# A load-and-store-bound SiLU-gate kernel: loads moved to the ACT ring, stores to the SP ring, with program order kept in every queue

## The chip, the cores and the metric

One core of one Trainium2 chip. The metric is the device time of one execution in microseconds (us), as the median of several runs. The profile's own span is about 1.8 us shorter than the time of the same run (470.1 against 471.92 us), so spans are compared with spans and times with times.

Words used below: SP, ACT and DVE are three engines of the core; in this kernel ACT computes the SiLU, DVE multiplies, and SP only issues transfers. A *ring* (or queue) is the list of transfers that one issuing engine feeds; here there are two, one fed by SP and one by ACT. A *piece* is one of the four 1 MB stores into which the last tile's output is cut. *Landing* is the moment when a transfer's completion is seen. Tiles are numbered 0 to 15, pieces 0 to 3.

## The reference

```python
batch, seq, dim = (32, 512, 2048)                 # x: float32, 134.2 MB
x1, x2 = x[..., :1024], x[..., 1024:]
out = (x1 * (1 / (1 + np.exp(-x1))) * x2)         # float32, 67.1 MB
```

There is nothing to reuse: 134.22 MB must be read and 67.11 MB written.

## The kernel before

The rows are cut into 16 tiles of 1024 rows (128 partitions with 8 rows each). Two input buffers and two output buffers rotate. SP issues the loads and ACT the stores. ACT computes SiLU of the left half, DVE multiplies by the right half, in four chunks per tile. The last tile's store is cut into four pieces so that it can start before the whole tile is done.

```python
    K = 8
    KC = 2
    # [cut: shapes, pools with bufs=2 for xt and for ot, views xv and ov]
    def load(i):
        xt = in_pool.tile([P, K, in_cols], dt, name="xt")
        nc.sync.dma_start(out=xt, in_=xv[i])
        loaded[i] = xt

    load(0)
    load(1)
    for i in range(n_tiles):
        xt = loaded.pop(i)
        last = i == n_tiles - 1
        ot = out_pool.tile([P, K, half], dt, name="ot")
        for c in range(0, K, KC):
            ce = c + KC
            nc.scalar.activation(                      # L56
                out=ot[:, c:ce, :],
                in_=xt[:, c:ce, :half],
                func=mybir.ActivationFunctionType.Silu,
            )
            nc.vector.tensor_mul(                      # L61
                out=ot[:, c:ce, :],
                in0=ot[:, c:ce, :],
                in1=xt[:, c:ce, half:],
            )
            if last:
                nc.scalar.dma_start(out=ov[i][:, c:ce, :], in_=ot[:, c:ce, :])   # L67
        if not last:
            nc.scalar.dma_start(out=ov[i], in_=ot)     # L69
        if i + 2 < n_tiles:
            load(i + 2)                                # L45
```

This order in the source is not the order on the engines: a scheduler places the instructions. In the built program the last tile stands on ACT as three activations, three store pieces, the fourth activation, the fourth piece.

## Time and profile before

| | before |
|---|---|
| time, median of 3 runs | 472.03 us (471.82 to 472.82) |
| span of the profiled run | 470.1 us |
| DVE busy, ACT busy | 30%, 25% of the span |
| period of one tile in the middle | 29.0 us |
| DMA rate in the middle | 434 GB/s |

From the page of the kernel before: busy time by engine, the DMA row of the timeline (tenths of 16 engines in 40 slices), the queues (packets, MB, share of the time of 16 engines), and the chain that ended last.

```profile
DVE 142.4 (30%) x64; ACT 118.3 (25%) x65; POOL 0.2 (0%) x4
...
DMA  8999999999999999999999999999999999999998
...
q1 hardware_dynamic: 2304, 134.22, 66.2%
q10 hardware_dynamic: 2736, 67.11, 33.1%
q14 instruction: 2, 0.02, 0.0%
...
DMA 80%; DVE 15%; ACT 4%; issue 0%; ACTq 0%; SPq 0%
```

Two queues with 66.2% and 33.1% add up to 99.3%: the 16 DMA engines have work for all but about 3 us of the span. q1 carries the loads (134.22 MB) and belongs to SP, q10 the stores and belongs to ACT.

The view by stretches of the kernel before (columns: stretch, its length, busy time of DVE, ACT and POOL with counts, clock, DMA share, GB/s):

```profile
58.00:116.00 58.00, 17.80 (x8) 14.62 (x8) 0.00 (x0) 1.00 1.00 434
...
290.00:348.00 58.00, 17.80 (x8) 14.62 (x8) 0.00 (x0) 1.00 1.00 434
...
452.00:470.10 18.10, 8.99 (x4) 7.42 (x4) 0.00 (x0) 1.00 0.84 357
```

In the middle the DMA engines move 434 GB/s with share 1.00. The Trainium skill, "DMA: Bandwidth & Descriptors", section "Where 436 GB/s comes from", states a fabric ceiling of 435 GB/s; the 434 GB/s measured here lie just under it. After the first 58 us (414 to 419 GB/s) there is slack only once the last load has landed (452 us).

The timeline of that tail, kernel before (start us, length, engine, line, operation; in brackets the idle time before it and what ended it):

```profile
452.05 5.51 ACT L56 ACTIVATE ot<-xt 128x2048 f32<-128x2048 f32 x3 [21.65 <-DMA xt<-in_x_dram]
453.99 6.70 DVE L61 TENSOR_TENSOR ot<-ot,xt 128x2048 f32<-128x2048 f32 x3 [20.06 <-ACT ot L56]
456.32 4.74 ACTq L67 DMA_DIRECT2D out_dram<-ot  x3
461.11 1.91 ACT L56 ACTIVATE ot<-xt 128x2048 f32<-128x2048 f32 x1 [3.54 <-DVE ot L61]
463.05 2.29 DVE L61 TENSOR_TENSOR ot<-ot,xt 128x2048 f32<-128x2048 f32 x1 [2.36 <-ACT ot L56]
465.37 0.34 ACTq L67 DMA_DIRECT2D out_dram<-ot  x1
```

The fourth activation stands behind the third store piece, and that piece waits for the third multiply. So ACT idles 3.54 us and DVE 2.36 us in the last tile.

The same view by quarter microseconds around the end of piece 2 (kernel before):

```profile
464.75:465.00 0.25, 0.25 (x1) 0.00 (x0) 0.00 (x0) 1.00 1.08 459
465.00:465.25 0.25, 0.25 (x1) 0.00 (x0) 0.00 (x0) 1.00 0.48 197
465.25:465.50 0.25, 0.09 (x1) 0.00 (x0) 0.00 (x0) 1.00 0.23 98
465.50:465.75 0.25, 0.00 (x0) 0.00 (x0) 0.00 (x0) 1.00 0.16 66
465.75:466.00 0.25, 0.00 (x0) 0.00 (x0) 0.00 (x0) 1.00 0.08 33
466.00:466.25 0.25, 0.00 (x0) 0.00 (x0) 0.00 (x0) 1.00 0.55 229
```

There is a hole from 465.1 to 466.2 us, before the data of piece 3 start. In the packet records the first of the 16 engines is done with piece 2 at 465.00 us and the last at 466.14, and they all start piece 3 between 466.21 and 466.36. So the first engine idles for 1.2 to 1.4 us, the last for 0.1 to 0.2.

### The profile page before, as it was taken

The page shows a single profiled execution, that of the slowest core. Times are in us where ns is not written, and L with a number is a line of the kernel's source. Part 1 is how long each engine was busy: PE and PEld are TensorE (multiplying, and loading weights), DVE is VectorE, ACT ScalarE, POOL GpSimd, SP SyncE. Part 2 cuts the span into 40 slices and gives each one's busy share as a digit, 9 for nine tenths or more (in the row PEclk, how much of TensorE's full clock was granted, in tenths as well). Part 3 has the DMA queues.
Part 4 walks back from the last instruction along what each step waited for, and adds up shares of the span by engine and source line. Part 5 has one row for each costly group of instructions (what it writes and reads, how often), then busy time and mean ns, then how long its engine had stood idle before and what let it go on. Part 6 is the DMA issues. An engine that isn't in the chain of part 4 may idle for free.

```text
span 470.1 us, 267 instructions
## 1 busy us (share of the span) xinstructions
DVE 142.4 (30%) x64; ACT 118.3 (25%) x65; POOL 0.2 (0%) x4
## 2 busy tenths in 40 slices
DVE  0070704207052070511606115070250702407033
ACT  1050506014060240602306032060320604106041
POOL 0000000000000000000000000000000000000000
DMA  8999999999999999999999999999999999999998
GB/s 357 446 446 401 401 485 435 418 401 443 449 446 401 441 457 396 446 474 390 468 404 438 457 441 407 427 420 449 446 410 432 480 401 418 440 474 424 399 424 337
DMA packets 5042, 201.35 MB, mean 428 GB/s; under 512 B 560, under 2 KB 560, under 8 KB 560
## 3 DMA queue, kind: packets, MB, share of 16 engines
q1 hardware_dynamic: 2304, 134.22, 66.2%
q10 hardware_dynamic: 2736, 67.11, 33.1%
q14 instruction: 2, 0.02, 0.0%
HBM read 134.22 MB, written 67.11 MB: 428 GB/s over the span
## 4 chain that ended last, share of the span: by engine, by line
DMA 80%; DVE 15%; ACT 4%; issue 0%; ACTq 0%; SPq 0%
DMA xt<-in_x_dram 80%; DVE ot L61 15%; ACT ot L56 4%; SPq L45 0%; ACTq L67 0%; ACTq L56 0%
## 5 line engine op out<-in xcount | busy, mean ns | idle before, releaser
L61 DVE TENSOR_TENSOR ot<-ot,xt 128x2048 f32<-128x2048 f32 x64 | 142.4, 2286 | 322.9 <-ACT ot L56 322.9
L56 ACT ACTIVATE ot<-xt 128x2048 f32<-128x2048 f32 x64 | 117.1, 1898 | 344.0 <-DMA xt<-in_x_dram 340.4
L56 ACT ACT_TABLE_LOAD x1 | 1.3, 1283 | 0.7 <-PEq L86 0.7
L86 POOL MEMSET const-bfloat16-1.0<- 128x1 bf16 x1 | 0.1, 101 | 0.0
L86 POOL MEMSET const-uint8-127<- 128x1 uint8 x1 | 0.1, 101 | 0.0
L86 POOL MEMSET const-float32-0.0<- 128x1 f32 x1 | 0.1, 98 | 0.2 <-issue 0.2
L86 POOL MEMSET const-float32-1.0<- 128x1 f32 x1 | 0.1, 98 | 0.0
## 6 DMA issues: line engine op xcount, KB each, us to landing
out_dram<-ot ACTq DMA_DIRECT2D x15, 4096.0 KB, 39.7
out_dram<-ot ACTq DMA_DIRECT2D x4, 1024.0 KB, 5.4
xt<-in_x_dram SPq DMA_DIRECT2D x16, 47.1
```

What stands on the lines that cost most here:

```text
L56: nc.scalar.activation(out=ot[:, c:ce, :], in_=xt[:, c:ce, :half], func=mybir.ActivationFunctionType.Silu,)
L61: nc.vector.tensor_mul(out=ot[:, c:ce, :], in0=ot[:, c:ce, :], in1=xt[:, c:ce, half:],)
L86: nc = _bacc.Bacc("TRN2", target_bir_lowering=False, num_devices=1)
```

## The change: its intent and the diff

Intent: ACT, which would otherwise be held by the last tile's stores, issues the loads instead (all issued by then), and SP issues the stores. The scheduler is switched off (`manual_schedule`), so each queue keeps program order, and the last tile's pieces follow on the store ring without holding ACT. The `PLAN` code is a general form of the same tiling; with this plan every tile still has 8 rows per partition.

```diff
-    n_tiles = num_rows // (P * K)
+    PLAN = [K] * (num_rows // (P * K))
 [cut: plan and view() compute the same row ranges from PLAN]
+    ctx.enter_context(tc.manual_schedule())
     def load(i):
         xt = in_pool.tile([P, K, in_cols], dt, name="xt")
-        nc.sync.dma_start(out=xt, in_=xv[i])
+        nc.scalar.dma_start(out=xt[:, :plan[i][1], :], in_=view(x_flat, i))
 [cut: unchanged compute]
             if last:
-                nc.scalar.dma_start(out=ov[i][:, c:ce, :], in_=ot[:, c:ce, :])
+                nc.sync.dma_start(out=ov[:, c:ce, :], in_=ot[:, c:ce, :])
         if not last:
-            nc.scalar.dma_start(out=ov[i], in_=ot)
+            nc.sync.dma_start(out=ov, in_=ot[:, :k, :])
```

More of the change, by code (lines that the diff above doesn't have):

```diff
@@ L31, with view @@
     KC = 2
-    n_tiles = num_rows // (P * K)
-    assert n_tiles * P * K == num_rows
+    PLAN = [K] * (num_rows // (P * K))
     in_pool = ctx.enter_context(tc.tile_pool(name="in_pool", bufs=2))
     out_pool = ctx.enter_context(tc.tile_pool(name="out_pool", bufs=2))
-    xv = x_flat.rearrange("(n p k) d -> n p k d", p=P, k=K)
-    ov = out_flat.rearrange("(n p k) d -> n p k d", p=P, k=K)
+    plan = []
+    row = 0
+    for k in PLAN:
+        plan.append((row, k))
+        row += P * k
+    assert row == num_rows
+    n_tiles = len(plan)
+    def view(flat, i):
+        row0, k = plan[i]
+        return flat[row0:row0 + P * k].rearrange("(p k) d -> p k d", k=k)
+    ctx.enter_context(tc.manual_schedule())
     loaded = {}
@@ L50 @@
     for i in range(n_tiles):
+        k = plan[i][1]
         xt = loaded.pop(i)
         last = i == n_tiles - 1
+        ov = view(out_flat, i)
         ot = out_pool.tile([P, K, half], dt, name="ot")
-        for c in range(0, K, KC):
-            ce = c + KC
+        for c in range(0, k, KC):
+            ce = min(c + KC, k)
             nc.scalar.activation(
```

## The prediction

> **What bounds the kernel now.** The 16 DMA engines. The view by stretches gives a DMA share of 1.00 and 434 GB/s in every 58 us pair of tiles from 58 to 406 us. DVE is busy 30%, ACT 25% (the page, part 1); the chain of waits is 80% load transfers. The Trainium skill, "DMA: Bandwidth & Descriptors", section "Where 436 GB/s comes from", gives a fabric ceiling of 435 GB/s; this trace sits on it. So only time in which the DMA engines have nothing to move can be won: about 1 us at the start, and something after the last load lands (452.0 us); from there to 470.1 the mean is 357 GB/s.
>
> **What the change moves.** The order of instructions on each engine shows loads going from SP to ACT and stores from ACT to SP, each still released by the fourth multiply of a tile (in the trace, load and store are issued at 405.10 and 405.11 us). No new wait is real: each store waits for its completion slot of four tiles earlier, long landed. An issue costs 0.33 us on SP, 0.36 us on ACT; ACT then idles about 21 us per tile for its load, so this is hidden. The same page, section "Issuing engines are not separate DMA queues", says that DMAs of either engine run on the same 16 engines; the steady state should keep 29.0 us per tile, loads landing in 47.1 us and stores in 39.6 us, the two queues' bytes exchanged.
>
> **Where it changes something: the last tile.** Before, ACT runs three activations, holds in the three store issues (456.32 to 461.06 us; the third waits for DVE) and starts its fourth activation at 461.11. So the last multiply ends only at 465.34. After, ACT runs four activations straight and SP issues the pieces: DVE multiplies back to back (8.91 us, as for other tiles) and ends at about 462.9, 2.4 us earlier. Not all of that counts: after the last load the store queue still holds the rest of tile 14's store, and the view by quarter microseconds shows the DMA engines full from 458 to 465.1 with that and the first three pieces. Only the hole from 465.2 to about 466.05 us, before the last piece's data starts, can close. That piece then moves from about 465.2 to 467.7 (2.4 to 2.6 us for 1 MB), with the same 1.4 us from last data to the end. Gain: 0.9 to 1.1 us, 0.2%; it would be 2.4 us if DMA were free there.
>
> **Predicted time:** 471.0 us (before 472.03), 8 in 10 between 469.6 and 472.4. Chances: faster by over 2% 0.01, within 2% 0.97, slower by over 2% 0.02.
>
> **What would show it right or wrong.** Right: 434 GB/s in the middle; span about 469.1; no wait of ACT for DVE in the last tile; last multiply ending near 462.9; last piece about 5.3 us from issue to landing (now 3.9), because it queues; no hole in DMA before it. Wrong: load landings away from 47.1 us, or another middle rate (then the rings are not alike, or not shared evenly); a first load starting later than 1.15 us.
>
> **What would make it wrong.** If the rings do not share the engines alike, the last load lands earlier or later than 452 us. Later by up to about 2 us would be absorbed, since the pieces would then come at DVE's pace; more would cost one for one. If the slow DMA engines' ends overlap better without the hole, the gain could reach 1.5 us. A middle rate different by 1% would move the time by over 4 us, more than all of this.

## The result, and the profile after

| | before | after |
|---|---|---|
| time, median of 4 runs each, same rounds | 472.16 us | 471.63 us (471.49 to 472.36) |
| ratio, 95% interval | | 0.999 (0.9973 to 1.0008): same |
| repeat on another occasion (11 and 5 runs) | 471.95 us | 471.30 us; ratio 0.9987 (0.9975 to 0.9999) |
| span of the profiled run | 470.1 us | 469.9 us |
| last multiply ends | 465.34 us | 462.84 us |
| last piece lands | 469.22 us | 469.03 us |

A ratio is the mean time of one kernel's fast runs over that of the other's of the same rounds, so it is not quite the ratio of the medians.

From the page after: the queues have exchanged their bytes and nothing else.

```profile
q10 hardware_dynamic: 2304, 134.22, 66.3%
q1 hardware_dynamic: 2736, 67.11, 33.1%
```

The view by stretches after: the middle is the same to the digit.

```profile
58.00:116.00 58.00, 17.79 (x8) 14.62 (x8) 0.00 (x0) 1.00 1.00 434
...
290.00:348.00 58.00, 17.79 (x8) 14.62 (x8) 0.00 (x0) 1.00 1.00 434
...
452.00:470.00 18.00, 8.90 (x4) 7.31 (x4) 0.00 (x0) 1.00 0.85 360
```

The tail's timeline after: four activations and four multiplies in one run each, no wait inside, SP issuing the pieces.

```profile
452.00 7.31 ACT L70 ACTIVATE ot<-xt 128x2048 f32<-128x2048 f32 x4 [21.48 <-DMA xt<-in_x_dram]
453.94 8.90 DVE L75 TENSOR_TENSOR ot<-ot,xt 128x2048 f32<-128x2048 f32 x4 [19.89 <-ACT ot L70]
456.26 6.94 SPq L81 DMA_DIRECT2D out_dram<-ot  x4
```

The quarter microseconds after, where the hole was and where the data end:

```profile
465.25:465.50 0.25, 0.00 (x0) 0.00 (x0) 0.00 (x0) 1.00 1.02 426
465.50:465.75 0.25, 0.00 (x0) 0.00 (x0) 0.00 (x0) 1.00 0.78 328
465.75:466.00 0.25, 0.00 (x0) 0.00 (x0) 0.00 (x0) 1.00 1.16 492
...
467.50:467.75 0.25, 0.00 (x0) 0.00 (x0) 0.00 (x0) 1.00 0.48 197
467.75:468.00 0.25, 0.00 (x0) 0.00 (x0) 0.00 (x0) 1.00 0.25 98
468.00:468.25 0.25, 0.00 (x0) 0.00 (x0) 0.00 (x0) 1.00 0.08 33
468.25:468.50 0.25, 0.00 (x0) 0.00 (x0) 0.00 (x0) 1.00 0.08 33
```

The hole is closed, as intended. But the engines do not end together at 467.7 us, as predicted: in the packet records the first has moved its last data at 467.55 us, 11 of the 16 by 467.91, and the last at 468.70 (the rows with share 0.08 hold one packet each). That last engine's packets follow each other without a gap from 465.3 us on.

The completion records of the trace show the same by engine. Each transfer counts 16 completions, one for each DMA engine that took part. First and last of the 16, in us:

| transfer | before: first, last | after: first, last |
|---|---|---|
| load of tile 15 | 450.72, 451.97 | 450.85, 451.98 |
| store of tile 14 | 457.98, 459.22 | 458.11, 459.23 |
| piece 0 | 460.45, 461.65 | 460.57, 461.68 |
| piece 1 | 462.89, 464.07 | 463.02, 464.17 |
| piece 2 | 465.33, 466.50 | 465.47, 466.59 |
| piece 3 | 469.07, 469.22 | 467.91, 469.03 |

Before, the leading engine gets from piece 2 to piece 3 in 3.74 us and the last one in 2.72. After, both take 2.44. So the first completion comes 1.16 us earlier, about the gain that I predicted, and the last one 0.19. (The records do not name the engine, so "leading" and "last" are places in the order of completion.) The Trainium skill, "DMA: Bandwidth & Descriptors", section "Why a DMA increments its semaphore by 16 and not by 1", states that the engines of a transfer finish independently and that only the full count means that all data have landed; this trace agrees, with 1.1 us between first and last. The kernel ends with the last.

### The profile page after: what moved, and what is told of

Read it like the earlier page. It is cut to its first block, busy times and chain, and to the rows that moved or that the text cites. A ratio compares the mean times of both kernels' runs of the same rounds, so it can differ in the third digit from the quotient of the medians.

```text
span 469.9 us, 269 instructions
## 1 busy us (share of the span) xinstructions
DVE 142.3 (30%) x64; ACT 118.2 (25%) x65; POOL 0.2 (0%) x4
## 4 chain that ended last, share of the span: by engine, by line
DMA 80%; DVE 15%; ACT 3%; DVEq 0%; issue 0%; ACTq 0%
DMA xt<-in_x_dram 80%; DVE ot L75 15%; ACT ot L70 3%; DVEq L111 0%; ACTq L57 0%
## 6 DMA issues: line engine op xcount, KB each, us to landing
xt<-in_x_dram ACTq DMA_DIRECT2D x16, 47.1
```

## The experiments

**Theory S.** The rings are alike. The end is the later of two things: the last of the 16 DMA engines working off its backlog, and the last multiply plus the landing of one lone piece (3.9 us). The change took 2.5 us off the second, but the first lies only 0.2 us before the old end, so it hides the rest. **Rival B**: the hole in the mean of the 16 engines is the gain (my prediction), 0.9 us and more. **Rival R**: the exchange of rings itself gives or costs something elsewhere.

### order_only: no exchange of rings, ACT not held

```diff
 # on the changed kernel: loads back on nc.sync, full stores back on nc.scalar
-            if last:
-                nc.sync.dma_start(out=ov[:, c:ce, :], in_=ot[:, c:ce, :])
+        if last:
+            for c in range(0, k, KC):
+                nc.scalar.dma_start(out=ov[:, c:c + KC, :], in_=ot[:, c:c + KC, :])
```

> Rings as before (loads SP, stores ACT); in the last tile ACT runs its four activations first and then issues the four store pieces. The first piece can be issued only at about 459.4 us instead of 456.3, its data start 0.7 us later, at 460.1. Theory S (what counts is the DMA engine that is furthest behind; in the changed kernel the engines finish tile 14's store between 457.6 and 458.7 us): that engine idles 1.4 us, so the last piece lands at about 470.3 and the span is about 471.2, +1.3 us on the changed kernel (469.9). Rival B (the hole of the bulk of the engines counts, as my prediction had it): they idle 2.5 us, last landing about 471.5, span about 472.4. Rival R (the rings themselves matter, order does not): span about 470.

Measured: 471.77 us against 472.03 (ratio 0.9993, 0.998 to 1.0005), span 469.9. The numbers of S and B did not come, because their premise was wrong: the first piece was not held until 459.4 us. R's "about 470" came, but this does not speak for R, since the changed kernel has the same span (469.9), and R says that order does not matter: the last multiply ends 10.92 us after the last load lands, as in the changed kernel (10.86), and not 13.37 us as before. The timeline of this run:

```profile
451.99 5.51 ACT L70 ACTIVATE ot<-xt 128x2048 f32<-128x2048 f32 x3 [21.56 <-DMA xt<-in_x_dram]
453.94 8.90 DVE L75 TENSOR_TENSOR ot<-ot,xt 128x2048 f32<-128x2048 f32 x4 [19.98 <-ACT ot L70]
456.26 0.34 ACTq L82 DMA_DIRECT2D out_dram<-ot  x1
457.41 1.89 ACT L70 ACTIVATE ot<-xt 128x2048 f32<-128x2048 f32 x1
458.46 4.74 ACTq L82 DMA_DIRECT2D out_dram<-ot  x3
```

The first piece is issued at 456.26 us, before the fourth activation *starts* (457.41), although it stands behind it in program order. The Trainium skill, "Perfetto Trace Analysis", section "DVE / Act Engine Instruction", says that the sequencer pushes a compute instruction into a queue and is then ready for the next one, and its section "DMA Instruction — HWDGE" puts a transfer's semaphore wait on the sequencer itself; this trace agrees with both. What holds ACT is therefore not the order "store before activation" as such, but a store that *waits* on the sequencer while later activations have not been pushed yet. With the four activations pushed first, ACT's own ring does as well as SP's: the last piece lands at 468.96 us. The run adds nothing to tell S from B, but it shows that the tail's gain does not need the exchange of rings.

### tail_only: only the four last pieces go to SP

```diff
 # on the changed kernel: loads on nc.sync, full stores on nc.scalar; the pieces stay on nc.sync
-        nc.scalar.dma_start(out=xt[:, :plan[i][1], :], in_=view(x_flat, i))
+        nc.sync.dma_start(out=xt[:, :plan[i][1], :], in_=view(x_flat, i))
-            nc.sync.dma_start(out=ov, in_=ot[:, :k, :])
+            nc.scalar.dma_start(out=ov, in_=ot[:, :k, :])
```

> Rings as before for loads and full stores; only the last tile's four pieces go to SP, so ACT is not held there. Last multiply ends near 462.9 us. Theory S (rings are alike, DMA engines never run dry): last landing 469.0, span 469.9, time 471.6 to 471.9 us, as the changed kernel. Rival R (the ring exchange costs or gives something elsewhere): span differs from the changed kernel by over 0.3 us, and the last load lands away from 452.0 us.

Measured: 471.91 us (ratio 0.9995, 0.9982 to 1.0007), span 470.1; the last load landed at 452.10 and the last piece at 469.14, 17.04 us later, against 17.05 in the changed kernel. Against R in the tail; the span is 0.1 us longer only because the last load landed 0.1 us later.

### late2, late3, late4: the last multiply moved later in steps

The fourth activation of the last tile is repeated, which gives the same values and costs ACT 1.94 us each time.

```diff
-            nc.scalar.activation(
+            for _ in range(3 if last and ce == K else 1):   # late3: 4, late4: 5
+                nc.scalar.activation(
```

> Changed kernel with the last tile's fourth activation repeated twice more (3.8 us of ACT), so that the last multiply ends at about 465.4 us, where it ended before the change. Theory S: last landing at the later of 469.0 and 3.9 us after that multiply: 469.3; span 470.2 us: no cost beyond the 0.2 us the profile shows between the two kernels. Rival B: 0.9 us on the changed kernel (span 470.8). Rival R: other than the span of before (470.1).

> The same with the fourth activation repeated three times more (5.7 us): last multiply ends at about 467.3. Theory S: past the hinge, one for one: last landing 471.2, span 472.1, +2.2 us on the changed kernel. Rival B: hole counted from 465.2, so 0.7 us more than that, span 472.8.

> Fourth activation of the last tile repeated four times more (7.6 us). Theory S: last multiply ends about 469.1 us, lands 3.9 us later (473.0), span 473.8, 1.9 us more than late3's 471.9: one for one past the hinge.

Measured: late2 472.43 us (ratio 1.0005, 0.9991 to 1.0019), span 470.2; late3 473.89 us (1.0039, 1.0023 to 1.0054), span 471.9; late4 476.23 us (1.0084, 1.0071 to 1.0098), span 474.4. The spans of late2 and late3 are those of S, within 0.2 us, and not those of B (470.8, 472.8). Late4 came out 0.6 us above the number, because the last multiply ended at 469.62 instead of 469.1; from there it follows the rule. The median of late2 is pulled up by two of its four runs (472.78, with spans of 471.0, which are nearer to B's number); only a run of span 470.2 was profiled, so this is not explained. In late3 all four spans (471.9 to 472.4) lie below B's 472.8.

### in_order: program order, rings not exchanged

```diff
 # on the changed kernel: loads on nc.sync, all stores and pieces on nc.scalar
-                nc.sync.dma_start(out=ov[:, c:ce, :], in_=ot[:, c:ce, :])
+                nc.scalar.dma_start(out=ov[:, c:ce, :], in_=ot[:, c:ce, :])
```

> Program order kept in each queue as in the change, but the rings not exchanged: loads SP, all stores ACT. In the last tile each activation then stands behind the store before it, which waits for its multiply. From the step seen in the kernel before (multiply ends 460.69, next multiply ends 465.34) the pieces come 4.65 us apart: last multiply ends at 470.2. Theory S: landing 3.9 us later, span 474.9, 5 us over the changed kernel. Rival R (only the scatter matters, or rings do): 470.

Measured: 476.99 us (ratio 1.0106, 1.0093 to 1.0119), span 475.6. Two steps of its timeline:

```profile
459.16 2.29 DVE L75 TENSOR_TENSOR ot<-ot,xt 128x2048 f32<-128x2048 f32 x1 [2.36 <-ACT ot L70]
461.48 0.34 ACTq L81 DMA_DIRECT2D out_dram<-ot  x1
461.87 1.91 ACT L70 ACTIVATE ot<-xt 128x2048 f32<-128x2048 f32 x1 [2.74 <-DVE ot L75]
463.81 2.29 DVE L75 TENSOR_TENSOR ot<-ot,xt 128x2048 f32<-128x2048 f32 x1 [2.36 <-ACT ot L70]
```

The multiplies come 4.65 us apart, as expected. The span is 0.7 us over the number, 0.5 of it because the last load landed late in this run (452.48). So with program order kept, the pieces must either go to SP's ring (changed kernel, tail_only) or be written behind the last activation (order_only): here each piece held the next activation.

### All tails together

Times after the landing of the last load, from the trace records (differences of the measured numbers, us):

| run | last multiply ends | last piece lands | landing minus multiply |
|---|---|---|---|
| changed kernel | 10.86 | 17.05 | 6.19 |
| after2 (repeat of it) | 10.86 | 16.95 | 6.09 |
| order_only | 10.92 | 17.05 | 6.13 |
| tail_only | 10.92 | 17.04 | 6.12 |
| kernel before | 13.37 | 17.25 | 3.88 |
| late2 | 13.54 | 17.41 | 3.87 |
| late3 | 15.47 | 19.33 | 3.86 |
| late4 | 17.42 | 21.31 | 3.89 |
| in_order | 18.28 | 22.15 | 3.87 |

This is a hinge: the piece lands at 17.0 us, or 3.88 us after the last multiply, whichever is later. The hinge lies at a multiply that ends 13.2 us after the load. The kernel before stood at 13.37, 0.2 us past it; the change moved it 2.3 us to the other side, where nothing more is won.

### free_before and free_after: the backlog taken away

The store of tile 14 is left out of each kernel, so that the store ring has no backlog when the pieces come. The result is wrong: those rows are not written.

```diff
-        if not last:
+        if i < n_tiles - 2:
```

> The kernel before without the store of the last tile but one (wrong on purpose: those rows are not written), so that the store queue is empty when the last tile's pieces come. Pieces then leave as soon as they are made. Theory S: the end follows the last multiply: it ends 13.4 us after the last load lands, its piece lands 3.9 us later, the span ends 0.9 us after that. To be compared with free_after.

> The changed kernel without the same store. Theory S: last multiply ends 10.9 us after the last load lands; the last piece queues some 0.2 us behind the third; so this is 2.2 us faster than free_before (against 0.2 us in the profiles with the store): the change's engine gain is real and is hidden only by the backlog. Rival R (rings or noise explain the small gain): the two differ by under 1 us.

Measured: 469.92 us and 468.28 us in the same rounds (ratios to the kernel before 0.9948, 0.9936 to 0.9961, and 0.9917, 0.9904 to 0.9931); spans 467.5 and 465.6. The change is worth 1.6 us in the times here, against 0.5 and 0.65 with the store. From the landing of the last load to that of the last piece it is 17.24 against 15.64 us. This contradicts R, and the direction is S's; the size was 2.2 us, and the term missed is the queueing of the pieces: they land 2.45 to 2.54 us apart while multiplies end 2.2 us apart, so the last piece takes 4.78 us from its multiply instead of 3.87. Without a backlog the 16 engines also finish within 0.2 us of each other.

### swap_only: rings exchanged, order left to the scheduler

```diff
-    ctx.enter_context(tc.manual_schedule())
```

> The rings exchanged, but program order not enforced: the scheduler then puts each later load on ACT behind the first two activations of the next tile, that is behind the landing of the load before it, so that one load is in flight at a time and not two. If the DMA engines go dry in that gap: several us per tile, up to 30 us in all. If the stores in the queue fill the gap (they have about 2 MB left when a load lands, an estimate from 4.19 MB and the 434 and 145 GB/s of the profile): 29 us per tile as before, span 470 to 471.5.

Measured: 486.73 us (ratio 1.0315, 1.0285 to 1.0345), span 483.7. Neither number: it is 14.8 us slower in the times, and a tile takes 29.76 us instead of 29.0. From the page of this run, the queues and the median time from a load's issue to its landing (47.1 us before):

```profile
q10 hardware_dynamic: 2304, 134.22, 66.9%
q1 hardware_dynamic: 2736, 67.11, 32.2%
...
xt<-in_x_dram ACTq DMA_DIRECT2D x16, 29.7
```

Its timeline, at the landing of two loads in succession:

```profile
407.66 1.91 ACT L69 ACTIVATE ot<-xt 128x2048 f32<-128x2048 f32 x1 [22.64 <-DMA xt<-in_x_dram]
407.71 0.33 ACTq L56 DMA_DIRECT2D xt<-in_x_dram  x1
...
437.42 1.91 ACT L69 ACTIVATE ot<-xt 128x2048 f32<-128x2048 f32 x1 [22.45 <-DMA xt<-in_x_dram]
437.48 0.33 ACTq L56 DMA_DIRECT2D xt<-in_x_dram  x1
```

Its view by stretches, over two of these periods:

```profile
377.97:407.71 29.74, 8.90 (x4) 7.10 (x5) 0.00 (x0) 1.00 1.00 421
407.71:437.48 29.77, 8.90 (x4) 7.32 (x5) 0.00 (x0) 1.00 1.00 420
```

A load is issued only after the one before has landed, as the order of instructions said. The stores do fill the gap: the DMA share stays at 1.00. And yet the rate is 420 instead of 434 GB/s. The queues' shares say where the time is: loads took 66.9% of 483.7 = 323.6 us, before 66.2% of 470.1 = 311.2, so 12.4 of the 13.6 us of span are load packets that took longer; stores took 155.8 and 155.6. In the packet records a load packet takes 2.42 us as a rule, but 2.6 to 3.8 us for many of them where a ring starts again beside the other: of the 324 such packets after the first 50 us, 273 start 0.9 to 6.7 us after a store is issued and 47 within 4 us after a load is issued. In the kernel before this happens once after the start, at 36 us, when the first store joins. That the restart costs this is read from where these packets lie; no run varies it alone, and the reason is open. Not exchanging rings, but taking the program-order lock away from the exchange, is thus the costliest of the variants run here: the exchange puts loads on ACT, and of these variants only those with `manual_schedule` keep them ahead of activations that wait.

### fewer and fewer2, after2: is there more to get?

```diff
-        for c in range(0, k, KC):
-            ce = min(c + KC, k)
+        step = KC if last else k
+        for c in range(0, k, step):
+            ce = min(c + step, k)
```

> The changed kernel with one activation and one multiply over a whole tile, except in the last tile (which keeps four): 45 fewer instructions on ACT and on DVE. In the traces so far two 8 KB instruction fetches of 0.31 us each run on DMA engines in mid-run (near 300 us) and the spread between first and last engine at a landing grows there. If the fetch is what sets the engine that is furthest behind, it disappears or moves, and the last landing comes 0.3 us earlier: span 469.6. If not: 469.9. Rival: later release of buffers (a tile's compute takes 16.7 us instead of 11) starves the queues: span over 471.

> The same kernel as fewer, on one chip with the changed kernel: its profile had no instruction fetch in mid-run and a span of 469.4 (0.5 us below the changed kernel), its times showed nothing. If the gain is real the median is 0.3 to 0.5 us below after2's; if not, equal within 0.2.

> The changed kernel unaltered, once more on one chip with the others of this set, because the runs so far do not tell its gain from the scatter of the runs (0.5 us). Theory S: 0.2 to 0.5 us below the kernel before; span of the profiled run 469.9.

Measured: fewer 472.13 us (ratio 0.9996, 0.9983 to 1.0008), span 469.4; fewer2 472.04 (1.0000, 0.9988 to 1.0012), span 469.4; after2 471.30 (0.9987, 0.9975 to 0.9999), span 469.5. The two instruction fetches in mid-run (0.31 us each, at 294.6 and 313.1 us in the changed kernel) are gone and the middle stays at 434 GB/s. The spread between first and last completion of a transfer stays between 0.77 and 0.84 us through fewer after its first load, while in the changed kernel it steps from 0.73 to 1.09 us across the second fetch. But the times do not follow: 472.04 is 0.7 us *above* after2 of the same set. Its times lie 2.2 us above its spans instead of 1.8, so part of it lies outside the span; the cause is open. Neither kernel beats the changed one, which has the lowest median of all correct kernels run here; its lead over order_only and tail_only (ratios 0.9987 against 0.9993 and 0.9995) lies within the intervals.

## Why the prediction was right or wrong

- **The time, 471.0 us (469.6 to 472.4), within 2%: right as a forecast.** Measured 471.63, in the repeat 471.30. The bound (DMA at 434 GB/s), the unchanged middle, the last multiply near 462.9 (462.84), no wait of ACT in the last tile and the closed hole were all seen. The range also holds 472.03, no change at all, so the time alone says little about the mechanism; the span named as a sign of being right, about 469.1 us, came out at 469.9.
- **The size of the gain, 0.9 to 1.1 us: too large.** The profiled spans differ by 0.2 us, the medians by 0.53 and in the repeat by 0.65. The interval of the repeat (0.9975 to 0.9999) is a gain of 0.05 to 1.2 us, so the times alone do not rule out the predicted gain; the landings in the profiles do, for the tail.
- **The step that failed** is "Only the hole from 465.2 to about 466.05 us, before the last piece's data starts, can close", taken as worth its full length. It was read from the mean over 16 engines. The leading engine did gain 1.16 us; the last one, which had data to move until 466.14 us, gained 0.19. The term measures 0.2 us, not 0.9.
- **The last piece's 5.3 us from issue to landing measured 6.2** (462.87 to 469.03), for the same reason: it has landed only when the engine that is furthest behind has worked off its queue.
- **"It would be 2.4 us if DMA were free there"**: with the backlog removed it was 1.6 us, since the pieces then queue behind each other (they land about 0.3 us further apart than the multiplies end).
- **"If the rings do not share the engines alike"**: they do. The middle ran at 434 GB/s and loads landed in 47.1 us, with the old rings and the new ones.
- **What the prediction did not ask** is whether the exchange is needed. It is not: order_only reaches a span of 469.9 us with the old rings. The exchange is one of three ways run here to keep program order without holding ACT (in_order costs 5 us without any of them), and it depends on the order being locked (swap_only, 14.8 us).
- **Still open:** between the 0.2 us of the profile pair and the 0.53 and 0.65 us of the times. The last load lands anywhere from 451.59 to 452.48 us in the profiles of kernels that are alike up to there; with the exchanged rings (changed kernel, after2, late2 to late4) the mean is 451.86, with the old ones (before, order_only, tail_only, in_order) 452.12. That would be 0.26 us, but the scatter within each group is as large, so it is not shown. The scatter lies almost wholly in how far the last engine lags: the first completion of that load comes at 450.72 to 450.90 us in all nine, and the last one 0.8 to 1.6 us later.

## What to carry to other kernels

When the last transfer of a kernel is backlogged, ask when the *last* DMA engine runs dry, not when the mean share falls: here a share of 0.08 was one engine at work, and the end waited for it. Take a tail apart as "backlog" and "last compute plus one lone landing"; removing time from the one that is not later wins nothing beyond the difference. In these runs a store whose issue waited for DVE held the activations behind it (3.54 us in the kernel before, 2.74 us for each piece in in_order), so push the compute first, or issue from an engine that has nothing to compute; and when loads move to a compute engine, look at the built order, because a scheduler can put them behind a wait (swap_only).

## What the Trainium skill lacked or had wrong

- "DMA: Bandwidth & Descriptors" says that a transfer's engines finish independently, but not how far apart: here 0.6 to 1.6 us at the last load's landing in the eleven runs with steadily fed rings, 3.4 us in swap_only, and about 0.2 us for pieces that came after the engines had run empty. Under a backlog the spread carries over from one transfer to the next (1.13 us at the last load, 1.12 us at the last piece of the changed kernel).
- The same page, section "Issuing engines are not separate DMA queues", says that using several issuers only saves issue time. For exchanging two steadily fed rings this held. It has nothing on rings that run empty in turn: in swap_only the rate was 420 instead of 434 GB/s at a DMA share of 1.00, with load packets of 2.6 to 3.8 us instead of 2.42 where a ring starts again beside the other (that the restart is the cause is inferred, not shown).
- "Perfetto Trace Analysis" has the push of compute instructions ahead of their execution, but no page draws the consequence for stores on ACT: a piece placed behind four activations was issued 1.15 us before the fourth one started, while a piece placed before an activation held it for 3.5 us.
- None has what a lone 1 MB store issued from SP or ACT costs from the end of its multiply to landing: 3.86 to 3.89 us in six runs.
